# Cross-attention outputs in one score tile, the attention sink as a score column, and a new order of the output projection in a two-layer encoder

## The chip, the core and the metric

The kernel runs on one core of a Trainium2 chip. The time is the device time of one launch in microseconds (us). The core's engines are named as the profile names them: PE (TensorE, matrix multiplies and transposes; PEld is its weight load), DVE (VectorE), ACT (ScalarE), POOL (GpSimd) and SP (SyncE, which here issues nearly all DMAs). Each runs its own instruction stream in order; semaphores make one wait for another. Matrix multiplies write into PSUM, which has 8 banks of 128 partitions x 512 fp32.

## What is computed

The reference is a two-layer encoder on x of 1024 tokens x 1024 features, with 256 memory tokens. Each layer normalises its input, projects it once into all queries, keys, values and gates, runs attention groups, multiplies their outputs with SiLU gates, projects back and adds the residual. Layer 0 has a windowed group A (6 query heads, 2 key heads), a dense group B (6 and 2) and a cross-attention X into the memory (4 heads); layer 1 has a differential group C (6 heads, each with two score maps and a value twice as wide) and again X. A final normalisation follows. The part that the change touches most is the softmax with a sink in A, a learned logit per head that takes part in the softmax and has no value:

```python
    logits = jnp.where(valid[None, :, None, None], logits + bias, NEG_INF)
    sink_col = jnp.broadcast_to(sink.astype(jnp.float32).reshape(1, 1, KVH, G, 1, 1),
                                logits.shape[:-1] + (1,))
    p = jax.nn.softmax(jnp.concatenate([logits, sink_col], axis=-1), axis=-1)[..., :-1]
    out = jnp.einsum("bnkgqs,bnskd->bnqkgd", p.astype(v.dtype), vw)
```

## The kernel before

**Arithmetic.** Everything is fp32. Each operand of a projection is split into a high and a low part (`h`, `wh`, `wl` and so on), and a product is three matmuls, so most matmuls come in threes.

**PSUM.** The 8 banks are three rings (L215 to L222): `ps_s`, tag S, two tiles of 1024 columns (4 banks), for scores; `ps_t`, tag T, two tiles of 512, for transposes; `ps_a`, tag A, two tiles of 512, for accumulators. A new tile of a ring waits until the one two before it has been read out.

**Attention steps.** `run_steps` (L441) walks over a list of steps. A step takes a block of queries. `s1` writes scores into an S tile, takes the row extremum on DVE and the exponentials on ACT; `finish` divides by the row sums; `hop` copies the result by DMA from `e` to `er` (to have it in the rounded fp32 form); `s2` transposes `er` into T tiles, which ACT and DVE read out as `PTh` and `PTl`; `s3`, one step later in every pair, multiplies these with the values into an accumulator, which is read out, gated on POOL and stored. Between these parts `jobs.pull` puts in pieces of projections (`acc`, L297) that have nothing to do with the attention, as filling for PE. Scores are kept negated, so the row extremum is a minimum `mn` and exp has scale -1.

**X steps** (L570 to L634; 8 in each layer, two layers). One S tile `sx` holds four heads' scores. The odd step's `s3` is called for the head pair p=0; `s3b` is the same for p=1, with a pull between them. Each writes 8 matmuls into an A tile `ox` (L616), which ACT copies by halves (L621), DVE adds (L624) and POOL gates (L627).

**B steps** (L1040 to L1090; 48). The row minimum `mn` (L1059, DVE) is multiplied with the query's norm factor `rq` (L1063, DVE) and is then the bias `mr` of the exponential (L1064, ACT). A normalising multiply follows on POOL (L1068).

**A steps** (L1106 to L1195; 24). Each step takes two query blocks of 128 (j = 0, 1), each with a window of 384 keys, or 256 at the ends of the sequence (p = 0 and p = 3). Per block one fused DVE instruction adds the bias and takes the minimum, with the negated sink as its start value (L1132), and one exp with row sum follows (L1136). The sink's own exponential `es` is one ACT instruction for both blocks (L1139), and `finish` adds it to the row sums (L1141).

**Output projection** (`out_proj`, L1216; one per layer). It takes the 8 token tiles in the order of the table `ORD[l]`. Some tiles have been begun earlier as filling (the table `PRE`): in layer 0 tiles 2 to 5 have 24 matmuls of 48 left and tiles 6 and 7 have 12; in layer 1 tiles 2, 3 and 4 have 12 left; the others have all 48. The sums go into S tiles of 1024 columns, the last tile's into A banks (`pieces`). Then per tile: DVE adds the residual (L1274), ACT squares (L1275), DVE and POOL make the norm factor (L1283, L229), DVE scales (L1295). In layer 0 the result of a tile is transposed (`tx`, L344) after the next tile's matmuls; those of the second half of the sequence are followed by layer 1's projections (`acc`). In layer 1 it goes out by DMA.

**What sets the order.** The program is handed to a list scheduler, which chooses the order in which each engine runs its instructions, from dependencies and its own estimates. So an edit of a few lines moves instructions far from it too.

**Stages in time.** Up to 85 us: norms, transposes and first projections; 85 to 150: layer 0's X steps; 150 to 540: B and A steps; 545 to 596: output projection 0; 588 to 640: layer 1's first projections; 640 to 715: layer 1's X steps; 690 to 1180: C steps; 1180 to 1254: output projection 1.

The functions that the diff touches, with the line numbers of the profile:

Of the kernel before, what the change touches and what calls it, by code (L numbers as in the profile page):

```python
# [12 lines left out]
F32 = mybir.dt.float32  # L13
# [5 lines left out]
P = 128  # L19
# [11 lines left out]
CUTS = ((0, 4, 6, 8), (0, 4, 6, 7, 8))  # L31
LAG = 3
FAST = ("m0", "m1", "m2", "m3")
ORD = ((0, 1, 2, 3, 4, 5, 6, 7), (0, 1, 4, 2, 5, 3, 6, 7))
JORD = "xq0 m0 g6 m1 m2 g7 m3 bk bq0 bv bq1 g3 bq2 ak av aq0 g0 aq1 g4 g1 aq2 g5 g2".split()
NB0 = 1
PAT = "BBABBABBABBABBAA" * 4
# [118 lines left out]
def encoder_kernel(ctx, tc, A):  # L156
# [412 lines left out]
    def x_steps(M, X, gates, fill, qtile, ydst):  # L569
        steps = []  # L570
        for qb in range(8):
            st = Step()
            st.sub = qb % 2
            if st.sub == 0:
                grp = {}
            st.grp = grp
            e = [None]
            st.fill = fill

            def s1(qb=qb, e=e):  # L580
                kh, kl = X["kh"], X["kl"]
                Sp = ps_s("sx").rearrange("p (h m) -> p h m", h=4)
                for h in range(4):
                    qt, qc = qtile(h, qb)
                    qk(Sp[:, XPOS[h], :], qt, qc, kh[:, h, :], kl[:, h, :], 0, MEM)
                mn = stat("mn4", 4)
                nc.vector.tensor_reduce(out=mn, in_=Sp, op=ALU.min, axis=AX.X)
                et = new_e(M)
                ev = et.rearrange("p (h m) -> p h m", h=4)
                z = stat("z4", 4)  # L590
                for h in range(4):
                    nc.scalar.activation(ev[:, h, :], Sp[:, h, :], AF.Exp, bias=mn[:, h:h + 1],
                                         scale=-1.0, accum_out=z[:, h:h + 1])
                def finish():
                    rz = stat("rz4", 4)
                    nc.vector.reciprocal(rz, z)
                    for h in range(4):
                        nc.scalar.activation(ev[:, h, :], ev[:, h, :], AF.Copy, scale=rz[:, h:h + 1])
                    e[0] = et
                return finish  # L600
            st.s1 = s1
            st.hop = word_copy(M, e)
            st.s2 = dense_s2(M, e, st)
            if st.sub == 1:
                def s3(qb=qb, grp=grp, ps=(0,)):
                    v = X["v"]
                    ph, pl_ = grp["pt"]
                    for p in ps:
                        acc = ps_a("ox")
                        t = M.at.tile([P, 256], F32, tag="yt", name="yt", bufs=2)  # L610
                        for j in range(2):
                            h = 2 * p + j
                            n = 0
                            for kt in range(2):
                                for pt in (ph, pl_):
                                    nc.tensor.matmul(acc[:, j * 256:j * 256 + 256], v[:, kt, h, :],  # L616
                                                     pt[:, 2 * XPOS[h] + kt, :], start=(n == 0), stop=(n == 3))
                                    n += 1
                        for j in range(2):
                            a = slice(j * 64, j * 64 + 64)  # L620
                            nc.scalar.copy(t[a, :], acc[64 - j * 64:128 - j * 64, j * 256:j * 256 + 256])  # L621
                        for j in range(2):
                            a = slice(j * 64, j * 64 + 64)
                            nc.vector.tensor_tensor(out=t[a, :], in0=acc[a, j * 256:j * 256 + 256], in1=t[a, :],  # L624
                                                    op=ALU.add)
                        g = gates[6 + p][:, (qb - 1) * P:(qb + 1) * P]
                        nc.gpsimd.tensor_tensor(out=g, in0=t, in1=g, op=ALU.mult)  # L627
                    if qb == 7:
                        for m in ps:
                            store_y(ydst, m, gates[6 + m])  # L630
                st.s3 = s3
                st.s3b = lambda s3=s3: s3(ps=(1,))
                st.need3 = ("g6", "g7")
            steps.append(st)  # L634
        return steps
# [398 lines left out]
    if True:  # L1034
        def b_step(h, qb):
# [8 lines left out]
            def s1(h=h, qb=qb, e=e):  # L1044
# [15 lines left out]
                et = new_e(M)  # L1060
                z = stat("z")
                mr = stat("mr")
                nc.vector.tensor_tensor(out=mr, in0=mn, in1=rq[:, qb, h:h + 1], op=ALU.mult)  # L1063
                nc.scalar.activation(et, Sp, AF.Exp, bias=mr, scale=nrq[:, qb, h:h + 1], accum_out=z)  # L1064
                def finish():
                    rz = stat("rz")
# [42 lines left out]
    if True:  # L1109
        def a_step(h, p):  # L1110
# [5 lines left out]
            def s1(h=h, p=p, e=e):  # L1116
# [3 lines left out]
                    jobs.ensure("aq%d" % ((h + 1) // 2))  # L1120
                    load_q(Aq, aq_d, h + 1)
                Sp = ps_s("sa").rearrange("p (j c) -> p j c", j=2)
                et = new_e(M)[:, :768].rearrange("p (j c) -> p j c", j=2)
                mn = stat("mn2", 2)
                z = stat("z2", 2)
                for j in range(2):
                    qb = 2 * p + j
                    lo, hi = max(0, qb - 1) * P, min(8, qb + 2) * P
                    c = lo - (qb - 1) * P
                    n = hi - lo  # L1130
                    qk(Sp[:, j, c:c + n], Aq[h], qb * P, Ak["k"][h // 3], Ak["kl"][h // 3], lo, n)
                    nc.vector.tensor_tensor_reduce(out=et[:, j, c:c + n], in0=Sp[:, j, c:c + n],  # L1132
                                                   in1=abias[h][:, c:c + n], scale=1.0,
                                                   scalar=nsink[:, h:h + 1], op0=ALU.add, op1=ALU.min,
                                                   accum_out=mn[:, j:j + 1])
                    nc.scalar.activation(et[:, j, c:c + n], et[:, j, c:c + n], AF.Exp,  # L1136
                                         bias=mn[:, j:j + 1], scale=-1.0, accum_out=z[:, j:j + 1])
                es = stat("es", 2)
                nc.scalar.activation(es, mn, AF.Exp, bias=sinkb[:, h:h + 1], scale=1.0)  # L1139
                def finish():  # L1140
                    nc.vector.tensor_tensor(out=z, in0=z, in1=es, op=ALU.add)  # L1141
                    rz = stat("rz2", 2)
                    nc.vector.reciprocal(rz, z)
                    for j in range(2):
# [7 lines left out]
            st.s1 = s1  # L1152

            def hop(p=p, e=e):
                t = M.at.tile([P, 1024], F32R, tag="er", name="er", bufs=M.cfg["er"])[:, :768]
                a, b = (P if p == 0 else 0), (768 - P if p == 3 else 768)
                ef = e[0].rearrange("p j c -> p (j c)")
                dma(t[:, a:b].bitcast(F32), ef[:, a:b])
                e[0] = t.rearrange("p (j c) -> p j c", j=2)
# [56 lines left out]
    def out_proj(l, hT_next, stack):  # L1216
# [11 lines left out]
            return xr  # L1228

        def pieces(i):  # L1230
            if i < TT - 1:
                S2 = ps_s("po")
                return [(S2[:, 0:512], 0, 512), (S2[:, 512:1024], 512, 512)], [(S2, 0, 1024)]
# [354 lines left out]
```

## Time and profile before

| | |
|---|---|
| median of 3 runs | 1252.83 us (1251.51 to 1255.9) |
| profiled execution | 1255.58 us, of which the span from first to last instruction is 1253.8 us |
| PE busy | 1205.5 us (96% of the span) |
| DVE, ACT, POOL busy | 817.1, 640.2, 413.5 us (65%, 51%, 33%) |
| mean granted clock of PE | 0.996 |

Rows of the profile read as line, engine, operation, output <- inputs, shape, count, then busy time and mean duration of one, then the idle time of the engine just before such instructions and what ended it. Two matmuls that follow each other overlap, so the time from one start to the next is shorter than the listed duration. In a table of windows each engine stands with its busy time in that stretch, then PE's granted clock, the DMA share and GB/s. In the list of waits each row has the total, the number of times and the longest wait in us.

### The profile page before, as it was taken

The page shows a single profiled execution, that of the slowest core. Times are in us where ns is not written, and L with a number is a line of the kernel's source. Part 1 is how long each engine was busy: PE and PEld are TensorE (multiplying, and loading weights), DVE is VectorE, ACT ScalarE, POOL GpSimd, SP SyncE. Part 2 cuts the span into 40 slices and gives each one's busy share as a digit, 9 for nine tenths or more (in the row PEclk, how much of TensorE's full clock was granted, in tenths as well). Part 3 has the DMA queues.
Part 4 walks back from the last instruction along what each step waited for, and adds up shares of the span by engine and source line. Part 5 has one row for each costly group of instructions (what it writes and reads, how often), then busy time and mean ns, then how long its engine had stood idle before and what let it go on. Part 6 is the DMA issues. An engine that isn't in the chain of part 4 may idle for free. (4 is left out here: it accounts for less than half of the span.)

```text
span 1253.8 us, 19637 instructions
## 1 busy us (share of the span) xinstructions
PE 1205.5 (96%) x6806; PEld 999.2 (80%) x6806; DVE 817.1 (65%) x1545; ACT 640.2 (51%) x1395; POOL 413.5 (33%) x390
## 2 busy tenths in 40 slices
PE   5999999999998999998999999999999999999997
PEld 4887788888887787887888778788887878877876
DVE  5547666377778788746355865766667666678444
ACT  6249654256666766533157644444444454456322
POOL 5023456266666565403122212212122131223100
PEclk9999999999999999999999999999999999999999
DMA  6654444545365575466644334243342433445363
GB/s 252 198 187 149 155 168 150 171 155 201 148 224 191 210 246 186 154 203 213 185 163 144 125 107 120 93 143 108 105 137 76 136 115 118 144 151 189 129 211 118
DMA packets 96350, 199.90 MB, mean 159 GB/s; under 512 B 11478, under 2 KB 31190, under 8 KB 96252
## 3 DMA queue, kind: packets, MB, share of 16 engines
q1 hardware_dynamic: 96252, 198.65, 47.4%
q8 instruction: 54, 0.88, 0.3%
q14 instruction: 44, 0.36, 0.1%
HBM read 79.32 MB, written 31.47 MB: 88 GB/s over the span
## 5 line engine op out<-in xcount | busy, mean ns | idle before, releaser
L297 PE MATMUL acc<-h,wh 128*128 128x512 f32 x1536 | 499.1, 399 | 7.3 <-DVE yt L624 3.1
L297 PEld LDWEIGHTS acc<-h,wh 128*128 128x128 f32 x1536 | 283.2, 188 | 73.3 <-issue 13.4
L297 PE MATMUL acc<-h,wl 128*128 128x512 f32 x768 | 304.6, 397 | 1.8 <-POOL wl L241 1.8
L241 POOL TENSOR_TENSOR wl<-wr,wh 128x512 fp32r<-128x512 f32 x96 | 124.9, 1302 | 340.0 <-DVE wh L239 125.2
L316 DVE TENSOR_TENSOR PTl<-te,PTh 128x512 fp32r<-128x512 f32 x224 | 148.2, 687 | 131.2 <-ACT PTh L315 128.4
L1440 ACT ACTIVATE e<-e,mn 128x1024 f32<-128x1024 f32 x96 | 110.2, 1149 | 130.7 <-DVE mn L1437 127.5
L297 PEld LDWEIGHTS acc<-h,wl 128*128 128x128 f32 x768 | 144.8, 189 | 35.5 <-issue 4.4
L315 ACT CAST PTh<-te 128x512 fp32r<-128x512 f32 x224 | 124.9, 591 | 30.2 <-PE te L540 24.6
L1068 POOL TENSOR_TENSOR e<-e,rz 128x1024 f32<-128x1024 f32 x48 | 91.7, 1913 | 78.1 <-DVE rz L1067 66.7
L1437 DVE CUSTOM_DVE_ANT_0 e<-sc,toep 128x1024 f32<-128x1024 f32 x96 | 113.9, 1217 | 5.3 <-PE sc L1431 5.0
L540 PEld LDWEIGHTS te<-identr,er 128*128 128x128 f32 x896 | 91.8, 143 | 21.1 <-issue 4.1
L540 PE MATMUL te<-identr,er 128*128 128x128 f32 x896 | 100.0, 246 | 7.5 <-issue 3.2
L239 DVE CAST wh<-wr 128x512 fp32r<-128x512 f32 x112 | 59.1, 530 | 43.9 <-PE acc L297 14.4
L1064 ACT ACTIVATE e<-sb,mr,nrq 128x1024 f32<-128x1024 f32 x48 | 58.0, 1208 | 48.4 <-DVE mr L1063 33.9
L1449 DVE SCALAR_TENSOR_TENSOR e<-e,mr 128x1024 f32<-128x1024 f32 x48 | 76.2, 1588 | 1.3
L1464 PE MATMUL oc<-PTh,v 128*128 128x256 f32 x384 | 74.8, 288 | 0.3 <-DVE ckl L1333 0.3
L660 PE MATMUL po<-woh,yh 128*128 128x512 f32 (+1 forms) x172 | 65.9, 383 | 1.5 <-DVE x L1274 1.5
L660 PE MATMUL po<-woh,yl 128*128 128x512 f32 (+1 forms) x172 | 65.6, 381 | 0.0
L660 PE MATMUL po<-wol,yh 128*128 128x512 f32 (+1 forms) x172 | 65.5, 381 | 0.0
L1464 PEld LDWEIGHTS oc<-PTh,v 128*128 128x128 f32 x384 | 61.5, 192 | 0.7 <-DVE ckl L1333 0.6
L1059 DVE TENSOR_REDUCE mn<-sb 128x1 f32<-128x1024 f32 x48 | 58.4, 1216 | 5.1 <-PE sb L509 4.7
L318 ACT ACTIVATE yh<-yr 128x256 fp32r<-128x256 f32 (+2 forms) x56 | 24.0, 448 | 67.3 <-DMA yr<-ysc 38.5
(199 smaller groups left out, 2247.1 us busy)
## 6 DMA issues: line engine op xcount, KB each, us to landing
er<-e SPq DMA_DIRECT2D x112, 512.0 KB, 2.9
wr<-in_w_in SPq DMA_DIRECT2D x96, 256.0 KB, 2.8
ysc<-gy SPq DMA_DIRECT2D x16, 512.0 KB, 2.9
wor<-in_w_out SPq DMA_DIRECT2D x32, 256.0 KB, 3.5
cq<-sg SPq DMA_DIRECT2D x64, 128.0 KB, 2.6
ck<-sg SPq DMA_DIRECT2D x48, 128.0 KB, 2.3
er<-e SPq DMA_DIRECT2D x12, 384.0 KB, 2.8
xpsc<-xh SPq DMA_DIRECT2D x18, 256.0 KB, 2.5
```

The source lines that it names most:

```text
L239: nc.vector.tensor_copy(hi, raw)
L241: (nc.vector if fast else nc.gpsimd).tensor_tensor(out=lo, in0=raw, in1=hi, op=ALU.subtract)
L297: lastmm[0] = nc.tensor.matmul(acc, a, b[:, k, c0:c0 + n], start=(i == 0), stop=(i == 23))
L315: nc.scalar.copy(hi, src)
L316: return nc.vector.tensor_tensor(out=lo, in0=src, in1=hi, op=ALU.subtract)
L540: nc.tensor.transpose(to[:, i * P:(i + 1) * P], e[0][:, k * P:(k + 1) * P], idt)
L660: lastmm[0] = nc.tensor.matmul(acc, a, b, start=(start and n == 0), stop=(stop and n == 2))
L1068: nc.gpsimd.tensor_tensor(out=et, in0=et, in1=rz.to_broadcast([P, 1024]), op=ALU.mult)
L1437: nc.vector.tensor_tensor_reduce(out=et, in0=Sp, in1=toeps[h][:, w0:w0 + 1024], scale=1.0, scalar=BIG, op0=ALU.add, op1=ALU.min, accum_out ...
L1440: nc.scalar.activation(et, et, AF.Exp, bias=mn[:, m:m + 1], scale=-1.0, accum_out=z[:, m:m + 1])
L1449: nc.vector.scalar_tensor_tensor(out=es[0], in0=es[1], scalar=c, in1=es[0], op0=ALU.mult, op1=ALU.add)
L1464: nc.tensor.matmul(acc, V[:, kt, v, :], pt[:, kt, :], start=(n == 0), stop=(n == 23))
```

## The change

1. The table `ORD` gets another order of the token tiles for both layers, and the third tile in the order gets two A banks and not an S tile, so that it is read out in two halves.
2. In the X steps both head pairs' outputs go into one S tile `ox`, a half each. All 16 matmuls come first, then both halves are read out. `s3b` and the pull between are gone; the step that had them now pulls both pieces ahead of `s3`.
3. In the B steps `mr` is made on ACT (an activation with the per-row factor as scale) and not on DVE.
4. In the A steps the block in `e` gets one more column. ACT copies the negated sink there before the scores are read out: one copy of 128x2 where both windows end at the same column, two of 128x1 in the steps at the sequence's end (p = 3), 30 copies in all. The exp takes the column in, so its row sum has the sink's part. `es` and the addition to `z` are gone (24 each). The DMA of `hop` takes 769 columns and not 768.

In the changed kernel the lines up to L760 are moved by up to 3, the later ones by 2, and those behind the A steps by 5 to 8.

```diff
-ORD = ((0, 1, 2, 3, 4, 5, 6, 7), (0, 1, 4, 2, 5, 3, 6, 7))
+ORD = ((0, 1, 2, 6, 3, 7, 4, 5), (0, 1, 5, 2, 6, 3, 4, 7))
...
             if st.sub == 1:
-                def s3(qb=qb, grp=grp, ps=(0,)):
+                def s3(qb=qb, grp=grp):
                     v = X["v"]
                     ph, pl_ = grp["pt"]
-                    for p in ps:
-                        acc = ps_a("ox")
-                        t = M.at.tile([P, 256], F32, tag="yt", name="yt", bufs=2)
+                    S2 = ps_s("ox")
+                    for p in range(2):
+                        acc = S2[:, p * 512:p * 512 + 512]
                         for j in range(2):
...
+                    for p in range(2):
+                        acc = S2[:, p * 512:p * 512 + 512]
+                        t = M.at.tile([P, 256], F32, tag="yt", name="yt", bufs=2)
                         for j in range(2):
                             a = slice(j * 64, j * 64 + 64)
                             nc.scalar.copy(t[a, :], acc[64 - j * 64:128 - j * 64, j * 256:j * 256 + 256])
...
-                st.s3b = lambda s3=s3: s3(ps=(1,))
...
-                nc.vector.tensor_tensor(out=mr, in0=mn, in1=rq[:, qb, h:h + 1], op=ALU.mult)
+                nc.scalar.activation(mr, mn, AF.Identity, scale=rq[:, qb, h:h + 1])
                 nc.scalar.activation(et, Sp, AF.Exp, bias=mr, scale=nrq[:, qb, h:h + 1], accum_out=z)
...
-                et = new_e(M)[:, :768].rearrange("p (j c) -> p j c", j=2)
+                et = new_e(M)[:, :770].rearrange("p (j c) -> p j c", j=2)
...
+                ends = [(min(8, qb + 2) - qb + 1) * P for qb in (2 * p, 2 * p + 1)]
+                if ends[0] == ends[1]:
+                    nc.scalar.copy(et[:, :, ends[0]], nsink[:, h:h + 1].to_broadcast([P, 2]))
+                else:
+                    for j in range(2):
+                        nc.scalar.copy(et[:, j, ends[j]:ends[j] + 1], nsink[:, h:h + 1])
...
-                    nc.scalar.activation(et[:, j, c:c + n], et[:, j, c:c + n], AF.Exp,
+                    nc.scalar.activation(et[:, j, c:c + n + 1], et[:, j, c:c + n + 1], AF.Exp,
                                          bias=mn[:, j:j + 1], scale=-1.0, accum_out=z[:, j:j + 1])
-                es = stat("es", 2)
-                nc.scalar.activation(es, mn, AF.Exp, bias=sinkb[:, h:h + 1], scale=1.0)
                 def finish():
-                    nc.vector.tensor_tensor(out=z, in0=z, in1=es, op=ALU.add)
...
-                a, b = (P if p == 0 else 0), (768 - P if p == 3 else 768)
+                a, b = (P if p == 0 else 0), (769 - P if p == 3 else 769)
...
         def pieces(i):
+            if i == 2:
+                p = [(ps_a("po")[:, 0:512], c, 512) for c in (0, 512)]
+                return p, p
             if i < TT - 1:
```

What the scheduler makes of it stands in the order of the instructions. The first place is PE in layer 0's X steps, at the third pair. `ox` is the output of the attention, `acc` a projection, `te` a transpose of a finished step's `er`, and the numbers tell tiles apart. Before:

```order
L616 MATMUL ox_1440<-PTh_1247,xv_410 128x256
L616 MATMUL ox_1440<-PTl_1249,xv_410 128x256
L297 MATMUL acc_1492<-h_120,wh_1212 128x512
L297 MATMUL acc_1492<-h_121,wh_1212 128x512
L297 MATMUL acc_1492<-h_120,wl_1213 128x512
```

In the changed kernel:

```order
L616 MATMUL ox_1424<-PTh_1246,xv_410 128x256
L616 MATMUL ox_1424<-PTl_1248,xv_410 128x256
L297 MATMUL acc_1490<-h_121,wh_1197 128x512
L297 MATMUL acc_1490<-h_120,wl_1198 128x512
L793 MATMUL ssq_1406<-small_80,sq_1399 128x2 x4
L540 MATMUL te_1457<-identr_74,er_1278 128x128 x4
L540 MATMUL te_1464<-identr_74,er_1278 128x128 x4
```

The second pair's output (`ox_1440`) used to take the A bank whose turn the projection's `acc_1492` shares; now all of `ox_1424` is in an S tile, the projection has begun in the middle of it, and the transposes `te`, which stood ahead of the second pair's output, come behind it.

The second place is PE in layer 1, where the last X steps meet the first C steps. `sc` are the two score maps of a C step (m = 0, 1), each an S tile; the matmuls with `ckl` have 64 rows, and those of the two maps can run side by side. Before:

```order
L616 MATMUL ox_7922<-PTl_7809,xv1_6875 128x256
L540 MATMUL te_7941<-identr_74,er_7848 128x128 x4
L540 MATMUL te_7948<-identr_74,er_7848 128x128 x4
L1425 MATMUL sc_7967<-ck0_7494,cq_7734 128x512 x2
L1431 MATMUL sc_7967<-ckl_7496,cq_7734 128x512
L1425 MATMUL sc_7968<-ck1_7495,cq_7737 128x512 x2
L1431 MATMUL sc_7968<-ckl_7496,cq_7737 128x512
L1431 MATMUL sc_7967<-ckl_7496,cq_7734 128x512
L1431 MATMUL sc_7968<-ckl_7496,cq_7737 128x512
L297 MATMUL acc_7996<-h_6327,wh_7675 128x512
```

In the changed kernel, in two pieces five rows apart (the rows between are of `acc`):

```order
L616 MATMUL ox_7865<-PTh_7765,xv1_6835 128x256
L616 MATMUL ox_7865<-PTl_7767,xv1_6835 128x256
L1433 MATMUL sc_7924<-ck0_7454,cq_7693 128x512 x2
L1439 MATMUL sc_7924<-ckl_7456,cq_7693 128x512 x2
L297 MATMUL acc_7953<-h_6281,wl_7635 128x512
L297 MATMUL acc_7953<-h_6281,wh_7634 128x512
```

```order
L297 MATMUL acc_7953<-h_6281,wl_7641 128x512
L1433 MATMUL sc_7925<-ck1_7455,cq_7696 128x512 x2
L1439 MATMUL sc_7925<-ckl_7456,cq_7696 128x512 x2
L297 MATMUL acc_7953<-h_6281,wh_7640 128x512
L297 MATMUL acc_7953<-h_6282,wh_7640 128x512
```

Each of the two score maps now stands by itself, with a projection's matmuls between them, since `ox_7865` holds one of the two S tiles until it has been read out. Three C steps stand so in the changed kernel, one did before.

The third place is ACT at an A step followed by a B step. Before:

```order
L315 CAST PTh<-te 128x4x128
L1136 ACTIVATE e,z_3146<-e,mn_3145 128x384
L1136 ACTIVATE e,z_3146<-e,mn_3145 128x256
L1139 ACTIVATE es<-mn_3145,small 128x2
L437 COPY yt<-ob 64x256
L315 CAST PTa<-ta 128x3x128 x2
L1064 ACTIVATE e,z<-sb,mr,nrq 128x1024
```

In the changed kernel:

```order
L315 CAST PTh<-te 128x4x128
L1133 COPY e<-nsink 128x1 x2
L1144 ACTIVATE e,z_3136<-e,mn_3135 128x385
L1144 ACTIVATE e,z_3136<-e,mn_3135 128x257
L437 COPY yt<-ob 64x256
L315 CAST PTa<-ta 128x3x128 x2
L1065 ACTIVATE mr<-mn,rq 128x1
L1066 ACTIVATE e,z<-sb,mr,nrq 128x1024
```

`es` is gone, the sink's copies stand ahead of the two exps, and `mr` stands ahead of the dense step's exp.

More of the change, by code (lines that the diff above doesn't have):

```diff
@@ L628, in s3 @@
                     if qb == 7:
-                        for m in ps:
+                        for m in range(2):
                             store_y(ydst, m, gates[6 + m])
                 st.s3 = s3
-                st.s3b = lambda s3=s3: s3(ps=(1,))
                 st.need3 = ("g6", "g7")
@@ L1154, in hop @@
             def hop(p=p, e=e):
-                t = M.at.tile([P, 1024], F32R, tag="er", name="er", bufs=M.cfg["er"])[:, :768]
-                a, b = (P if p == 0 else 0), (768 - P if p == 3 else 768)
+                t = M.at.tile([P, 1024], F32R, tag="er", name="er", bufs=M.cfg["er"])[:, :770]
+                a, b = (P if p == 0 else 0), (769 - P if p == 3 else 769)
                 ef = e[0].rearrange("p j c -> p (j c)")
```

## The prediction

> **What bounds the kernel now.** I began with the busy time per 100 us, to see where PE has anything left to lose.
>
> ```profile
> 300.00:400.00 100.00, 97.73 (x602) 83.55 (x600) 75.87 (x172) 65.24 (x148) 63.07 (x59) 1.00 0.51 181
> 400.00:500.00 100.00, 92.74 (x570) 78.10 (x570) 81.66 (x178) 68.82 (x151) 58.97 (x52) 0.98 0.63 222
> 500.00:600.00 100.00, 95.19 (x514) 79.19 (x513) 62.03 (x117) 41.96 (x95) 28.58 (x32) 1.00 0.59 192
> 800.00:900.00 100.00, 100.00 (x564) 80.93 (x563) 69.28 (x121) 47.69 (x95) 21.60 (x22) 1.00 0.34 113
> ```
>
> After the two window bounds and their length comes PE. It is the bound everywhere; in the C steps (800 to 900) it is never idle, and the change leaves them alone. It can only give back PE's idle time elsewhere: 2.3 + 7.3 us between 300 and 500, 4.8 us around output projection 0, and some in the X steps. The list of PE's waits says what ends that idle time.
>
> ```profile
> PE te L540 <- issue: 3.2, 5, 1.4
> PE acc L297 <- DVE yt L624: 3.1, 2, 1.8
> PE sa L509 <- ACT e L1064: 2.1, 2, 1.1
> PE sa L509 <- DVE mn L1132: 1.7, 3, 1.1
> PE tx L344 <- DVE h L316: 1.7, 1, 1.7
> PE po L660 <- DVE x L1274: 1.5, 1, 1.5
> PE pre L660 <- DVE yt L438: 1.2, 1, 1.2
> PE tx L344 <- DVE xs L1295: 1.2, 2, 0.7
> PE acc L297 <- DVE v L1283: 1.1, 1, 1.1
> ```
>
> No wait is large. The change aims at several of these rows: `yt L624` (A banks in the X steps), `e L1064` (exponential of B behind `mr`), and the `po`, `tx` and `acc` rows of the output projections. All nine make 16.8 us: even with every one of them gone the kernel would be 1.3% faster.
>
> **Layer 0's X steps.** A projection's `acc` waits twice for an A bank that DVE (L624) has not read out. The change takes `ox` out of the A banks, so these 3.1 us have no cause left. But look at what ACT does there (fourth engine in the row, after PE, PEld and DVE), and how long the read-out lasts:
>
> ```profile
> 110.00:120.00 10.00, 8.75 (x54) 7.35 (x52) 6.59 (x14) 9.80 (x28) 1.47 (x2) 1.00 0.77 205
> 120.00:130.00 10.00, 8.92 (x62) 7.89 (x60) 7.36 (x13) 9.85 (x26) 7.66 (x6) 1.00 0.46 160
> 130.00:140.00 10.00, 9.26 (x39) 7.57 (x40) 5.03 (x11) 7.34 (x20) 1.97 (x2) 0.83 0.53 180
> 130.74 1.10 PE L297 MATMUL acc<-h,wh 128*128 128x512 f32 x2 [1.82 <-DVE yt L624]
> L621 ACT COPY yt<-ox 64x256 f32<-64x256 f32 x32 | 11.7, 367 | 0.7
> L624 DVE TENSOR_TENSOR yt<-ox,yt 64x256 f32<-64x256 f32 x32 | 13.4, 420 | 2.6 <-ACT yt L621 1.7 <-issue 0.5
> ```
>
> From 110 to 130 ACT idles 0.35 us. What runs through ACT (exponentials, divisions, `PTh`) cannot come sooner by more than that; PE can only run ahead with projections, and then meets the transposes `te` of a step whose division is not done. And the S ring now carries `ox` as well: an S tile with `ox` is held for four copies and four adds, 4 x 0.367 + 4 x 0.420 = 3.1 us if ACT and DVE do not overlap. So the bounds are a gain of 3.1 us and, with one read-out uncovered, a loss of 3.1 us. I take a gain of 1: the A-bank wait is certain to go, most of it should reappear at `te`.
>
> **B and A steps.** DVE loses 48 `mr` and 24 additions, ACT gets 48 `mr` and 30 sink copies and loses 24 `es`:
>
> ```profile
> L1063 DVE TENSOR_TENSOR mr<-mn,rq 128x1 f32<-128x1 f32 x48 | 9.3, 193 | 0.7
> L1141 DVE TENSOR_TENSOR z<-z,es 128x2 f32<-128x2 f32 x24 | 6.9, 286 | 14.0 <-ACT es L1139 13.9
> L1139 ACT ACTIVATE es<-mn,small 128x2 f32<-128x2 f32 x24 | 6.8, 281 | 0.0
> L1483 ACT ACTIVATE z<-ssqc,es 128x1 f32<-128x1 f32 x48 | 10.0, 258 | 4.5 <-PE ssqc L1479 4.3
> ```
>
> DVE is relieved of 9.3 + 6.9 = 16.2 us. No row has ACT's new operations; nearest is L1483, one column with a per-row operand, 0.258 us. That makes 48 x 0.258 + 30 x 0.258 - 6.8 = 13.3 us more on ACT. Over the 390 us of these steps DVE is the busier engine (76 and 82% against 65 and 69%), so the load moves the right way. One `mr` is 0.258 - 0.193 = 0.065 us dearer there, 48 x 0.065 = 3.1 us if every one lay on the path. [...]
>
> Whether a `mr` is on the path is decided by queues. DVE's in-order queue did this to one of them:
>
> ```profile
> 394.38 3.64 DVE L258 TENSOR_TENSOR wol<-wor,woh 128x512 fp32r<-128x512 f32 x1
> 397.94 0.15 DVE L1063 TENSOR_TENSOR mr<-mn,rq 128x1 f32<-128x1 f32 x1
> 398.12 1.21 ACT L1064 ACTIVATE e<-sb,mr,nrq 128x1024 f32<-128x1024 f32 x1 [2.48 <-DVE mr L1063]
> 399.47 0.44 PE L509 MATMUL sa<-ak,q 128*128 128x384 f32 x1 [0.98 <-ACT e L1064]
> 401.43 0.50 PE L540 MATMUL te<-identr,er 128*128 128x128 f32 x4 [1.35 <-issue]
> ```
>
> DVE had just taken the minimum, a weight split of 3.64 us came between it and `mr`, ACT stood idle for 2.48 us, and PE paid 0.98 us for the S tile that this exp held and, as I read it, 1.35 us behind it. With `mr` on ACT the exp no longer queues behind DVE's split. Against these 2.3 us stand the exps where ACT is the late one: each starts up to 0.26 us later. Three such on PE's path make 0.8. I take a gain of 1.5. Bounds: the five rows of waits of these steps (`te` 3.2, `sa` 2.1 and 1.7, `pre` 1.2) all gone, 8.2; or the 11 waits in them each longer by one `mr` and one copy, 11 x 0.52 = 5.7 lost. The sink's copies stand ahead of DVE's minimum on the same tile; ACT is normally free by then, and I cost them at nothing; were they late, they would be in these 5.7. `es` and its addition leave the division's chain, which ends in a DMA that PE meets a step later: nothing. The 769th column lengthens a DMA that lands steps ahead of its use: nothing.
>
> **Output projections.** The chain behind a tile, against a matmul's pitch (0.23 us between the first two starts):
>
> ```profile
> L1274 DVE TENSOR_TENSOR x<-po,xr 128x1024 f32<-128x1024 f32 (+2 forms) x19 | 20.0, 1053 | 17.5 <-PE po L660 13.4 <-issue 3.2 <-DMA x1sc<-x 0.8
> L1275 ACT ACTIVATE xs<-x 128x1024 f32<-128x1024 f32 (+1 forms) x16 | 16.1, 1008 | 14.8 <-DVE x L1274 7.8 <-DVE yl L319 3.5 <-issue 1.8
> L1295 DVE SCALAR_TENSOR_TENSOR xs<-x,r,gb 128x1024 f32<-128x1024 f32 (+1 forms) x16 | 20.0, 1251 | 10.5 <-POOL r L229 10.4
> 1209.32 0.39 PE L660 MATMUL po<-wol,yh 128*128 128x512 f32 x1
> 1209.55 0.39 PE L660 MATMUL po<-woh,yl 128*128 128x512 f32 x1
> 1211.43 0.47 PE L660 MATMUL po<-woh,yh 128*128 128x512 f32 x1 [1.49 <-DVE x L1274]
> ```
>
> From a tile's last matmul to its transposes lie at least 1.05 + 1.01 + 1.25 = 3.3 us and the small operations. A short tile (12 matmuls) covers 12 x 0.23 = 2.7 us, one of 24 covers 5.5, a full one 10.9. In layer 0 the two short tiles stood last, and 1.2 + 1.1 + 1.7 = 4.0 us of waits (`tx`, `acc`, `tx`) lie at this place. With the order 0, 1, 2, 6, 3, 7, 4, 5 the two tiles ahead of a short one (2 and 3) are still badly covered; the last one is now long, its first half is read out while the second runs, and layer 1's start has its bank. So the 1.1 us should go, and a little of the others: gain 1.4, bounds 0 and 4.0. In layer 1 two short tiles followed 0 and 1 directly, and the fifth waited 1.49 us for an S tile. Now the third is a full one in A banks, and every S tile that is reused has a long one or an idle DVE ahead: gain 1.5, bounds 0 and 1.5.
>
> **Layer 1, where X meets C.** A C step's 64-row matmuls cost less when those of two maps alternate:
>
> ```profile
> 690.03 0.73 PE L1431 MATMUL sc<-ckl,cq 64*128 64x512 f32 x2
> 690.69 0.50 PE L616 MATMUL ox<-PTh,xv 128*128 128x256 f32 x2
> 704.68 0.73 PE L1431 MATMUL sc<-ckl,cq 64*128 64x512 f32 x4
> 705.34 0.73 PE L297 MATMUL acc<-h,wh 128*128 128x512 f32 x2
> ```
>
> Two alone take 690.69 - 690.03 = 0.66 us, four alternating take the same 0.66. In the changed order three C steps are torn apart and not one: 2 x 0.66 = 1.3 us lost. The waits of the second map for `ox`'s read-out come on top, 0 to 3.1; the A-bank waits of these steps go, under 1. I take a loss of 0.5; bounds 1 gained, 4 lost.
>
> **The sum.** -1 - 1.5 - 1.4 - 1.5 + 0.5 = -4.9, against a profiled execution of 1255.58: 1250.7. That execution lay 2.75 above the median of 1252.83, so the median after is 1252.83 - 4.9 = 1247.9, 0.4% faster. About 0.3% (3.8 us, 1249.0) is what a measurement can tell from no change.
>
> **The rivals.** *The gains are given back.* ACT is the pacer in the X steps and PE waits at `te` for what it saved; in the B and A steps the earlier and the later exps cancel. Then only the output projections and the torn C steps count: -1.4 - 1.5 + 1.3 = -1.6, 1251.2. For it: ACT's 0.35 us of idle. Against it: DVE's queue at 394. If instead every `mr` on ACT is paid for on the path, the sum is without the 1.5 and with 3.1: 1247.9 + 1.5 + 3.1 = 1252.5; and if no edit does what it says, it stays at 1252.8. All three are within 0.3% and share one chance.
>
> *The clock.* One more row, beside 130 to 140 above:
>
> ```profile
> 430.00:440.00 10.00, 9.35 (x51) 7.85 (x51) 8.23 (x20) 7.48 (x17) 6.64 (x6) 0.83 0.71 247
> ```
>
> In both windows the granted clock is 0.83, which loses 10 x 0.17 = 1.7 us each, and one begins right behind the wait at 130.74. If the change removes both waits' idle time and makes no new one, 3.4 us more are gained: 1244.5. But the waits at 401 and 1211 drew no such drop, so it hangs on chance. [...]
>
> *Slower: a ring of two.* `ox` in the S ring leaves the scores one tile, in the steps that need it most; in six of the eight cross outputs (the first of each layer has no queue) the next scores or map wait for the read-out as long as the A-bank waits lasted, 3.1 / 2 = 1.55 us: 6 x 1.55 = 9.3. With the other terms (-1.5 - 1.4 - 1.5 + 1.3, -3.1) that is 1259. It decides from 3.1 / 6 = 0.5 us per output up. For it: ACT at 98%, the torn maps. Against: seven or more of a projection's matmuls (7 x 0.23 = 1.6 us) stand between in the order.
>
> **How the numbers follow.** Forecast 0.45 (1247.9, own range 1245 to 1251), gains given back 0.25 (1251.2), clock 0.14 (1244.5), ring 0.16 (1259). Faster by over 0.3%: three quarters of the forecast, the clock, a little of the second: 0.50. Slower: nearly all of the ring: 0.15. Within: 0.35. The range 1243 to 1256 leaves out the clock's lower end and most of the ring.
>
> **What would show it.** Right: no `acc <- yt L624` in the list of waits; the exp near 398 starts about 2 us earlier and `sa` behind it no longer waits; no wait of `po` near 1211; three pairs of 64-row matmuls at 0.66 us around 700. Wrong: PE waits of 1 us or more at `te` between 110 and 150 or at `sc` around 700; more waits `<- ACT e` in the B steps than the two of before; a granted clock below 1 in windows that had 1.

## The result, and the profile after

The changed kernel took 1242.89 us (median of 6 runs, 1241.58 to 1244.78) against 1254.37 us of the kernel before beside it (1251.51 to 1257.93): a ratio of 0.9910, 95% interval 0.9895 to 0.9925. In a later set on one chip the same two stood at 0.9893 (0.9877 to 0.9909). So it is 0.9 to 1.1% faster, on the side that was forecast and more than twice as far as the 0.4% of the forecast. The measured 1242.89 us is below the forecast's own range of 1245 to 1251 and 0.1 us below the lower end of the whole range, 1243 to 1256.

The profiled execution took 1241.79 us with a span of 1240.0, 13.8 us less than before. To see where, I counted PE's matmuls by their pitch and compared the two traces at equal amounts of work done. (Each kind of matmul counts with its usual time from one start to the next, its pitch. This is worked out from the records of one trace each; it leaves shifts of a few tenths, since the order differs.)

| stretch, by the clock of the kernel before | gain in the traces | forecast |
|---|---|---|
| 100 to 161 us: X steps of layer 0 | 5.6 us | 1.0 |
| 161 to 530: B and A steps | 2.7 | 1.5 |
| 530 to 640: output projection 0, first projections of layer 1 | 0.2 | 1.4 |
| 640 to 749: X steps of layer 1 into the C steps | 3.0 | -0.5 |
| 749 to 1173: C steps | 0.1 | 0 |
| from 1173: output projection 1 | 2.2 | 1.5 |
| sum | 13.8 | 4.9 |

The two stretches with X steps have 8.6 us of it, where 0.5 was expected. Of the 13.8 us, 10.5 are idle time of PE and 3.3 are busy time, which fell from 1205.5 to 1202.2. First the sums of the changed kernel, then its busy time per 100 us (PE is the first number behind the length):

```profile
PE 1202.2 (97%) x6806; PEld 999.9 (81%) x6806; DVE 805.7 (65%) x1479; ACT 651.9 (53%) x1453; POOL 412.1 (33%) x390
```

```profile
100.00:200.00 100.00, 99.57 (x585) 84.83 (x584) 67.17 (x114) 74.56 (x168) 50.40 (x41) 1.00 0.45 159
300.00:400.00 100.00, 97.52 (x608) 85.19 (x607) 76.75 (x149) 69.77 (x166) 66.03 (x59) 0.98 0.56 197
400.00:500.00 100.00, 93.25 (x576) 78.89 (x575) 77.08 (x156) 70.76 (x167) 59.26 (x52) 0.98 0.59 210
500.00:600.00 100.00, 96.39 (x501) 79.45 (x500) 57.97 (x103) 37.65 (x85) 22.93 (x28) 1.00 0.61 193
700.00:800.00 100.00, 99.46 (x549) 79.50 (x547) 66.36 (x122) 46.83 (x92) 23.02 (x23) 1.00 0.34 116
```

Between 300 and 500, PE is nearly as idle as it was (2.5 + 6.8 us, before 2.3 + 7.3). PE's list of waits in the changed kernel, by its longest rows behind the start-up:

```profile
PE tx L344 <- DVE xs L1303: 3.2, 5, 1.2
PE te L540 <- issue: 2.5, 1, 2.5
PE ob L1083 <- ACT PTh L315: 2.4, 1, 2.4
PE ob L1083 <- DVE PTl L316: 1.2, 2, 0.6
PE oa L1192 <- DVE yt L438: 1.1, 1, 1.1
```

`acc <- DVE yt`, `sa <- ACT e`, `po <- DVE x`, `acc <- DVE v` and `tx <- DVE h` are gone. In their place stand three rows that were short or absent: `tx <- DVE xs` (1.2 in 2 before), `ob <- ACT PTh` and `ob <- DVE PTl`. And this is the same stretch as the one that the prediction took for paced by ACT:

```profile
110.00:120.00 10.00, 9.69 (x60) 8.09 (x59) 7.03 (x14) 9.68 (x26) 3.76 (x5) 1.00 0.70 206
120.00:130.00 10.00, 10.00 (x69) 9.05 (x68) 6.90 (x11) 9.43 (x24) 4.00 (x4) 1.00 0.45 158
130.00:140.00 10.00, 10.00 (x54) 7.84 (x52) 7.76 (x16) 8.73 (x25) 2.78 (x3) 1.00 0.43 160
```

ACT is still 94 to 97% busy up to 130, and PE is idle for 0.3 us of these 30, where it was idle for 3.1. The granted clock is 1.00 at 130, where it was 0.83.

### The profile page after: what moved, and what is told of

The parts are those of the page before. It is cut to its first block, busy times and chain, and to the rows that moved or that the text cites. A ratio compares the mean times of both kernels' runs of the same rounds, so it can differ in the third digit from the quotient of the medians.

```text
span 1240.0 us, 19680 instructions
## 1 busy us (share of the span) xinstructions
PE 1202.2 (97%) x6806; PEld 999.9 (81%) x6806; DVE 805.7 (65%) x1479; ACT 651.9 (53%) x1453; POOL 412.1 (33%) x390
## 5 line engine op out<-in xcount | busy, mean ns | idle before, releaser
L239 DVE CAST wh<-wr 128x512 fp32r<-128x512 f32 x112 | 56.3, 504 | 42.1 <-PE acc L297 17.8
```

## The experiments

### Which part is worth how much

The first set undoes one part or does one alone. Undoing the second part (the cross outputs back into the A banks, one call per head pair):

```diff
-                    S2 = ps_s("ox")
-                    for p in range(2):
-                        acc = S2[:, p * 512:p * 512 + 512]
+                    for p in ps:
+                        acc = ps_a("ox")
...
+                st.s3b = lambda s3=s3: s3(ps=(1,))
```

> All of the change except its second part: the cross outputs stay in the A banks, one call per head pair. Theory 1 (by the stages of the two traces: the X steps of layer 0 gave 5.6 us and those of layer 1 some 2 to 3): without it 8 us of the 11.5 are gone, about 1251, ratio to the kernel before 0.997, and the two waits of the projection for the A bank (1.25 and 1.82 us) and a granted clock below 1 near 130 us are back. Theory 2 (the prediction's: ACT paces the X steps, so this part is worth 0.5 us and the rest came from elsewhere): about 1243.5, ratio 0.991 to 0.992.

Measured: 1249.77 us, ratio to the kernel before 0.9956 (0.9942 to 0.9971). So the part is worth 0.9956 - 0.9910, 0.46% or 5.8 us. Theory 2 falls, and the 8 us of Theory 1 were too much. In the trace against the kernel before, the stretch of layer 0's X steps has gained 1.6 us by 188 us (the full change: 5.8), and layer 1's, from 640 to 749, 1.4 (full: 3.0). Both waits for the A bank are back, at the same places, but the clock is not:

```profile
117.03 0.70 PE L297 MATMUL acc<-h,wh 128*128 128x512 f32 x2 [1.24 <-DVE yt L624]
130.90 0.70 PE L297 MATMUL acc<-h,wh 128*128 128x512 f32 x2 [1.82 <-DVE yt L624]
```

```profile
130.00:140.00 10.00, 9.10 (x47) 7.65 (x48) 5.68 (x11) 7.88 (x21) 2.06 (x3) 1.00 0.52 170
```

The same idle times 0.2 us later than in the kernel before, and 1.00 where that one had 0.83. So the drop at 130 us does not follow from the wait alone, and the 1.6 us by which this kernel is ahead there fit its absence (1.7 us). Without the clock the part is worth 5.8 - 1.6 = 4.2 us in layer 0: the 3.1 us of the two waits and about 1 more, whose cause no row shows.

The second part alone, put into the kernel before (the diff of point 2 and nothing else):

> The kernel before with only the second part: the cross outputs in one S tile per pair of steps. Theory 1: 8 us faster than the kernel before, about 1246, ratio 0.993 to 0.994, no wait of the projection for the A bank, clock 1.0 from 100 to 200 us. Theory 2 (worth 0.5 us): ratio 0.999 to 1.000. A third way: the gain needs the other parts, because the scheduler orders the whole differently; then the ratio lies between and the stage to 150 us alone shows the gain.

Measured: 1247.65 us, ratio 0.9938 (0.9915 to 0.9962), 7.8 us faster. Theory 1. In the trace it has gained 5.9 us by 188 us and 2.6 from 640 to 749; output projection 1 gave nothing (7.4 us ahead at 1173, 7.2 at 1227), where the full change and the first experiment gained 2.1 over the same stretch.

The third part undone (`mr` back on DVE):

```diff
-                nc.scalar.activation(mr, mn, AF.Identity, scale=rq[:, qb, h:h + 1])
+                nc.vector.tensor_tensor(out=mr, in0=mn, in1=rq[:, qb, h:h + 1], op=ALU.mult)
```

> All of the change except its third part: the product for the dense steps' exponential stays on DVE. Theory 1: the queue of DVE was what cost PE 0.98 and 1.35 us near 400 us, so 1 to 2.5 us come back: about 1244.5, ratio to the kernel before 0.992 to 0.993. Rival: ACT's 48 x 0.26 us cost more on the path than DVE's queue, so this kernel is faster than the full change, ratio 0.989 or less. Third: no difference beyond the interval, 0.991, since the scheduler fills PE with projections either way.

Measured: 1243.92 us, ratio 0.9911 (0.9890 to 0.9932). The third expectation: no difference from the full change that these intervals can tell.

The fourth part undone (`es` and its addition back, no sink column):

```diff
-                    nc.scalar.activation(et[:, j, c:c + n + 1], et[:, j, c:c + n + 1], AF.Exp,
+                    nc.scalar.activation(et[:, j, c:c + n], et[:, j, c:c + n], AF.Exp,
...
+                nc.scalar.activation(es, mn, AF.Exp, bias=sinkb[:, h:h + 1], scale=1.0)
...
+                    nc.vector.tensor_tensor(out=z, in0=z, in1=es, op=ALU.add)
```

> All of the change except its fourth part: the windowed steps keep the sink's own exponential and its addition, and no sink column. Theory 1: the part saves 24 x (0.28 + 0.29) us on ACT and DVE, costs 30 copies on ACT, and is off PE's path: ratio 0.990 to 0.992 as the full change. Rival: the shorter chain behind the windowed exponentials is worth 1 to 2 us of the B and A stage's 2.4: ratio 0.992 to 0.993.

Measured: 1242.05 us, ratio 0.9897 (0.9876 to 0.9919). Theory 1 in that nothing is lost; the ratio lies just below its range.

### Both of these together, and the output projections

Parts 3 and 4 both undone (the last two diffs):

> The kernel before with parts 1 and 2 alone (new tile order with the third tile in A banks, cross outputs in score tiles); the product stays on DVE and the sink keeps its exponential. Theory 1 (the runs with one of them undone lay at 0.9911 and 0.9897, the full change at 0.9910): parts 3 and 4 together are worth 0 to 1 us, ratio to the kernel before 0.990 to 0.992. Rival (the B and A stage gained 2.3 us between the two traces, and that is theirs): ratio 0.9925 to 0.993.

Measured: 1243.64 us, ratio 0.9913 (0.9896 to 0.9929), in Theory 1's range: parts 3 and 4 together are worth between nothing and 2 us (0.9913 against 0.9910 in one set and 0.9893 in another), and the intervals do not settle where. PE's waits from 300 us to the end of the A steps got no shorter. Without the two parts:

```profile
PE te L540 <- issue: 2.6, 4, 1.3
PE sa L509 <- ACT e L1066: 2.0, 2, 1.0
PE pre L662 <- DVE yt L438: 1.2, 1, 1.2
PE oa L1189 <- DVE yt L438: 0.9, 1, 0.9
```

All rows of that answer add up to 8.4 us, those of the full change in the same stretch to 9.2. But the count of matmuls from 161 to 530 us tells the kernels apart: the ten traces with `mr` on ACT gain 1.0 to 3.2 us there over the kernel before, the three with `mr` on DVE (this one, the one with only the third part undone and the one with the second part alone) -1.0 to 0.4. So the third part seems to be worth about 2 us in this stretch, in shorter times between matmuls and not in the listed waits; no row shows through what. The fourth part shows no gain there (2.8 and 3.0 in the two traces without it).

In the list of waits, the one for the exponential goes and others come. The trace of the full change shows how, at the step that stood at 398 in the kernel before. First ACT, then DVE, then PE:

```profile
385.90 0.30 ACT L1065 ACTIVATE mr<-mn,rq 128x1 f32<-128x1 f32 x1
386.28 1.21 ACT L1066 ACTIVATE e<-sb,mr,nrq 128x1024 f32<-128x1024 f32 x1
```

```profile
383.98 1.22 DVE L1061 TENSOR_REDUCE mn<-sb 128x1 f32<-128x1024 f32 x1
385.11 4.57 DVE L258 TENSOR_TENSOR wol<-wor,woh 128x512 fp32r<-128x512 f32 x2
389.60 0.15 DVE L1069 RECIPROCAL rz<-z 128x1 f32<-128x1 f32 x1
391.12 1.27 DVE L316 TENSOR_TENSOR PTl<-te,PTh 128x512 fp32r<-128x512 f32 x2
```

```profile
391.89 0.51 PE L540 MATMUL te<-identr,er 128*128 128x128 f32 x4 [2.48 <-issue]
```

The minimum is done at 383.98 + 1.22 = 385.20 and the exp starts 1.1 us later, where it had taken 3.7 us: that is what the third part is there to do. But two weight splits still hold DVE for 4.57 us, and now the reciprocal and, behind an addition and the next minimum, the low parts `PTl` in the same queue are what is late. The transposes start when the first of the two `PTl` is done, near 391.12 + 1.27 / 2 = 391.8; that they waited for it is read from the times, since the row names no releaser. PE idles 2.48 us there in one piece, where it had idled 0.98 + 1.35 in two.

The old order of tiles in layer 0's output projection, with its third tile in an S tile again, everything else as in the full change:

```diff
-ORD = ((0, 1, 2, 6, 3, 7, 4, 5), (0, 1, 5, 2, 6, 3, 4, 7))
+ORD = ((0, 1, 2, 3, 4, 5, 6, 7), (0, 1, 5, 2, 6, 3, 4, 7))
...
-            if i == 2:
+            if i == 2 and l == 1:
```

> The full change, but layer 0's output projection keeps the old order of tiles and its third tile in an S tile; layer 1's is the new. Theory 1 (by the two traces this place nets 0 to 0.8 us: one wait of 1.1 us for a bank went, and the waits at the transposes for the scaled tile grew from 1.2 in 2 to 3.2 us in 5): ratio 0.990 to 0.9915. Rival (the prediction's 1.4 us): ratio 0.992 to 0.9925.

Measured: 1243.57 us, ratio 0.9913 (0.9896 to 0.9931): Theory 1. The old waits are back,

```profile
PE tx L344 <- DVE h L316: 1.6, 1, 1.6
PE tx L344 <- DVE xs L1303: 1.1, 2, 0.7
PE acc L297 <- DVE v L1291: 1.1, 1, 1.1
```

3.8 us in place of the new order's 3.2 at the transposes: layer 0's new order is worth about half a microsecond, below what can be told.

The third tile of both output projections in an S tile, the new orders kept:

```diff
-            if i == 2:
-                p = [(ps_a("po")[:, 0:512], c, 512) for c in (0, 512)]
-                return p, p
```

> The full change, but the third tile of both output projections is in an S tile as before; the new orders stay. Theory 1 (the order alone does it: no short tile follows another with a reused S tile): no wait of po over 1 us, ratio 0.990 to 0.9915. Rival (the A banks are needed): the third tile is a full one and starts right behind the last 6 matmuls (1.4 us) of the second, while the first one's S tile needs 1.2 us of read-out and more; 0.5 to 2 us are lost in each layer, ratio 0.992 to 0.9935, with a po wait of that size.

Measured: 1241.71 us, ratio 0.9895 (0.9876 to 0.9914), and no `po` wait in the trace: Theory 1, a little below its range. The order does it; the A banks for the third tile are not needed.

### Where the gain of the X steps comes from

The score tile in layer 0 alone, layer 1's cross outputs in the A banks:

```diff
+                if ydst == 0:
                     def s3(qb=qb, grp=grp):
...
+                else:
+                    def s3(qb=qb, grp=grp, ps=(0,)):
...
+                    st.s3b = lambda s3=s3: s3(ps=(1,))
```

> The full change, but layer 1's cross outputs stay in the A banks; layer 0's are in score tiles. Theory 1 (the second part gains in both layers, in layer 1 by 1.6 to 2.8 us in the traces): ratio 0.9923 to 0.9932. Rival (the prediction's: in layer 1 it tears two more pairs of score maps apart at 0.66 us each and lends S tiles away, so without it the kernel is faster): ratio 0.990 or less, with the paired 64-row matmuls back.

Measured: 1245.08 us, ratio 0.9925 (0.9910 to 0.9940), against 0.9910 and 0.9893 for the full change: 1.9 to 4 us. The first of these intervals overlaps this run's, the second ends just below it. In the trace it loses 2.4 us to the full change from 640 to 749. Theory 1. The whole list of PE's waits in that stretch:

```profile
PE te L540 <- DVE v L316: 1.7, 1, 1.7
PE ox L648 <- ACT e L598: 0.6, 1, 0.6
PE ox L648 <- DVE yt L656: 0.6, 2, 0.3
```

The kernel before has the same three, 2.4 us in all, the last two shorter,

```profile
PE te L540 <- DVE v L316: 1.7, 1, 1.7
PE ox L616 <- DVE yt L624: 0.5, 2, 0.3
PE ox L616 <- ACT e L598: 0.2, 1, 0.2
```

and the full change has none of them. It does pay for the torn pairs of score maps as predicted: three of its C steps have the 64-row matmuls of each map alone, 0.66 us for two:

```profile
683.53 0.73 PE L1439 MATMUL sc<-ckl,cq 64*128 64x512 f32 x2
684.19 0.39 PE L616 MATMUL ox<-PTh,xv 128*128 128x256 f32 x1
```

So against this run 2.9 us of waits go and 1.3 come, as two more pairs are torn than in the kernel before: 1.6, of the 2.4 in the trace.

Then a set with the full change on the same chip, which stood there at 1241.45 us, 0.9893 (0.9877 to 0.9909):

> The changed kernel once more, so that the three others of this set have it on the same chip. All theories: ratio to the kernel before 0.990 to 0.992. Near 130 us the granted clock is 1; whether a window between 300 and 500 us is at half clock may differ from the first profile, if the drops hang on when a wait falls and not on the kernel alone.

As expected, and with drops of the clock at the same two places as in its first profile. Beside it, ACT's copies of layer 0's cross outputs done twice, to ask whether ACT paces that stage:

```diff
+                            for _ in range(2 if ydst == 0 else 1):
-                            nc.scalar.copy(t[a, :], acc[64 - j * 64:128 - j * 64, j * 256:j * 256 + 256])
+                                nc.scalar.copy(t[a, :], acc[64 - j * 64:128 - j * 64, j * 256:j * 256 + 256])
```

> The full change with each of ACT's 16 half-tile copies of layer 0's cross outputs done twice (the same values, 16 x 0.37 = 6 us more on ACT between 100 and 150 us, and each score tile held 0.7 us or more longer). Theory 1 (PE has projections to run and the S tile is free long before it is needed; ACT does not pace the stage): at most 1 us lost, ratio 0.990 to 0.992. Rival (the prediction's: ACT is busy 98% and paces the stage): 4 to 6 us lost, ratio 0.994 to 0.9955, with PE waits at the transposes or scores between 100 and 150 us.

Measured: 1245.60 us, ratio 0.9929 (0.9913 to 0.9945), 4.1 us more than the full change on the same chip. Neither expectation holds whole: more is lost than Theory 1 allows, and the rival has the loss and a wait for a score tile right, but not the ratio. By the traces 1.9 us of it are lost in the stage itself, out of 16 x 0.37 = 6 us added; so ACT does not set the pace of the stage, though it is not far from it. The rest is lost behind 400 us, where by the names of the tiles each engine runs the order of the full change (the orders differ only between 112 and 172 us); its cause stays open. In the stage PE now waits once for a score tile:

```profile
119.03 0.35 PE L509 MATMUL sx<-xkh,q 128*128 128x256 f32 x1 [1.17 <-ACT e L592]
118.03 0.86 DVE L628 TENSOR_TENSOR yt<-ox,yt 64x256 f32<-64x256 f32 x2 [1.46 <-ACT yt L625]
```

The first row names an exponential as the releaser, but the additions that read `ox` out of this tile end at 118.03 + 0.86 = 118.89, 0.14 us before the matmul. This is the ring of two of the slower rival. It begins to bite when the tile is held longer; in the full change it does not. There the tile that `ox` left at 108 us is read out by 115.3 and needed at 119.8 (PE, ACT, DVE, PE):

```profile
108.01 0.28 PE L616 MATMUL ox<-PTl,xv 128*128 128x256 f32 x1
```

```profile
113.61 0.75 ACT L624 COPY yt<-ox 64x256 f32<-64x256 f32 x2
```

```profile
114.39 0.86 DVE L627 TENSOR_TENSOR yt<-ox,yt 64x256 f32<-64x256 f32 x2
```

```profile
119.78 0.28 PE L509 MATMUL sx<-xkh,q 128*128 128x256 f32 x1
```

So there is 4.5 us of slack (1.6 us at the least among layer 0's four outputs), and the read-out, whose second half begins 5.6 us after the matmuls, holds up nobody.

Last of this kind, the halves of the one S tile called one after the other again, each with its own read-out and a pull between:

```diff
-                def s3(qb=qb, grp=grp):
+                def s3(qb=qb, grp=grp, ps=(0,)):
-                    S2 = ps_s("ox")
+                    if 0 in ps:
+                        grp["ox"] = ps_s("ox")
+                    S2 = grp["ox"]
...
+                st.s3b = lambda s3=s3: s3(ps=(1,))
```

> The full change, but the two head pairs are called one after the other as before, each with its own read-out and a projection piece between them; both still use the halves of one S tile. Theory 1 (the gain comes from taking the outputs out of the A banks): ratio 0.990 to 0.992. Rival (the gain comes from doing all 16 matmuls at once and from the merged pull): 3 to 7 us lost, ratio 0.9935 to 0.9965.

Measured: 1247.38 us, ratio 0.9939 (0.9924 to 0.9953), 5.9 us more than the full change beside it. Each theory has one half. In layer 0's X steps almost nothing is lost (0.2 us by 161), so there the gain comes from leaving the A banks. In layer 1 4.0 us are lost from 640 to 749, more than with A banks; 2.3 of them are waits that the full change does not have, at `ox` (1.0 and 0.3) and at `te` (1.0). About 1 us more is lost between the two stretches, with no cause shown. PE, and the DVE additions it waits for:

```profile
660.50 0.36 PE L619 MATMUL ox<-PTh,xv 128*128 128x256 f32 x1 [1.00 <-ACT e L598]
```

```profile
659.50 0.86 DVE L627 TENSOR_TENSOR yt<-ox,yt 64x256 f32<-64x256 f32 x2 [0.59 <-ACT yt L624]
```

The second pair's matmuls start at 660.50, right after the additions that read out the first pair's half, at 659.50 + 0.86 = 660.36. The row names an ACT instruction of the division as the releaser, which does not touch this tile; the additions end 0.14 us before the matmul starts. The two halves are different banks but one tile, and the second half waited here until the first had been read out: in all eight pairs of this trace its matmuls start 0.14 us or more behind these additions. In the kernel before, with an A tile for each, two of the eight start ahead of them (127.81 against 130.59, and 692.02 against 694.33). With all 16 matmuls first there is nothing to wait for. Whether the two pulls put together have a share in layer 1's gain, no run separates.

### A version to beat both

The full change without its sink column and with the third tile in an S tile (the diffs above):

> The full change without its sink column and with the third tile of the output projections in an S tile. Theory 1 (both were neutral or slightly faster alone, 0.9897 and 0.9895): ratio 0.988 to 0.990, 1 to 2 us faster than the full change on the same chip. Rival (both differences were chance): 0.9905 to 0.992 as the full change.

Measured: 1242.28 us, ratio 0.9900 (0.9884 to 0.9915), beside the full change's 0.9893: no faster than the full change on the same chip, as the rival had it, though both ratios are below the rival's range. Neither is faster than the other, and no version of these runs is told apart from the full change on the good side.

## Why the prediction was right in sign and too small

**What bounds the kernel** stood: PE, with the C steps untouched (0.1 us over 420 us). What the list of waits allowed (16.8 us) was not passed; 11.5 us is well below. But it was not the limit that it was taken for: 3.3 of the profile's 13.8 us came out of PE's busy time, which no wait lists. Of the signs named beforehand all four for "right" came, and one of the three for "wrong": a lower clock in a window that had 1, at 390.

**Layer 0's X steps: the step that failed.** The prediction took 1 of 3.1 us, because "what runs through ACT cannot come sooner by more than that" and the wait "should reappear at `te`". It did not. The changed kernel's trace has no `te` wait in that stage, and PE was filled with projections. 4.2 us are measured for the part without the clock (the first experiment against the full change), all of the two waits and 1 us more. The false step is to read ACT's busy share as a pace. ACT's queue held work that was urgent only while the output sat in an A bank; once it sits in a tile with 1.6 us of slack or more the copies can come late. The doubled copies show the size: of 6 us more on an engine called full, 1.9 were lost in the stage.

**The clock** was a rival of its own at 0.14, and its 1244.5 is the nearest of the named times to the 1242.89 measured. That is chance. Of its two places one came true: the drop at 130 us is gone in every kernel with the score tile there, 1.7 us (and in the first experiment, which has the old wait). But the other, near 430, stayed and a new one came near 390, behind the 2.48 us wait of `te`: two drops before, two after. So the clock moved within the sum and gave nothing net. It also makes the B and A stretch, with one drop more than before, look 1.7 us worse than it would at full clock.

**B and A steps.** 1.5 was taken, with 0 to 2 us found for parts 3 and 4 by the times and about 2 for the third by the traces, so the size was about right. The way to it was not. DVE's split ahead of `mr` was seen rightly, and the exp no longer queues behind it; but the instructions behind `mr` in the same DVE queue stay late, and the 2.3 us that PE should have won near 398 came back as 2.48. By the count, the gain lies in shorter times between matmuls, which the prediction did not look at, and their cause is open. (Its "five rows" of waits are four; their sum of 8.2 is right.) `mr` itself costs more on ACT than the 0.258 us assumed, the copies less:

```profile
L1065 ACT ACTIVATE mr<-mn,rq 128x1 f32<-128x1 f32 x48 | 14.1, 295 | 42.4 <-DVE mn L1061 42.0
L1130 ACT COPY e<-nsink 128x2 f32<-128x2 f32 x18 | 3.5, 201 | 0.4 <-DMA er<-e 0.4
L1133 ACT COPY e<-nsink 128x1 f32<-128x1 f32 x12 | 1.8, 200 | 0.0
```

14.1 + 3.5 + 1.8 - 6.8 = 12.6 us more on ACT, 13.3 were estimated. One `mr` takes 0.295 us on ACT, where it took 0.193 on DVE. On which of the two it belongs the times do not settle: with `mr` on DVE the kernel ran at 0.9911, within the interval of the full change (0.9895 to 0.9925). The count of matmuls (1.0 to 3.2 us gained with `mr` on ACT, -1.0 to 0.4 with it on DVE) speaks for ACT in this case.

**Output projections.** Layer 1's term was right in cause and place: the `po` wait went by the order, 2.1 us with what came behind it, 1.5 forecast. Layer 0's term failed: the `acc` wait of 1.1 went as said, but "a little of the others" did not go with it; the `tx` waits grew to 3.2 us, so 0.6 or less was left of 1.4. And of the two means in this part, the A banks for the third tile were not needed.

**Layer 1, where X meets C.** The torn pairs cost their 1.3 us, as worked out. The other side of that term was mis-sized: the waits that the change takes away here were put at "under 1". They were 1.7 (`te <- DVE v`), which I had quoted and then given to nobody, and 0.7 at `ox`. And no wait for a torn map's tile came. So the loss of 0.5 should have been a gain of 1.7 + 0.7 - 1.3 = 1.1 by these rows; the traces show 1.6 to 3.0 (3.0 against the kernel before, 2.4 and 1.6 against the two runs with layer 1's outputs in A banks), outside the bound of 1 gained, and the rest has no row.

**The rivals.** "Gains given back" held for layer 0's order and for the waits of the B and A steps, not for the whole. The ring of two did not decide: PE stood idle for no score tile in the full change, and the doubled copies brought one such wait of 1.2 us.

## What to carry to other kernels

A busy share near 100% on an engine did not make it the pace-setter of a stage here (ACT, 94 to 97% busy in the full change, was given 6 us more, and 1.9 were lost): ask which of its instructions somebody waits for, and whether a tile that is needed again later lets the others come late. A wait that is quoted has to be given a fate in the sum, gone or kept, also where the change seems to be about something else. Moving one short instruction out of a long in-order queue freed what hung on it (the exp starts 1.1 us behind the minimum, where it took 3.7) and left the next one in that queue to be waited for (2.48 us of PE's time); and the second half of one tile waited for the first, 1.0 us at 660.50, even in different banks, so write both before reading either.

## What was not expected of the hardware

PE's clock drops (0.83 to 0.84 in a window of 10 us, 3.4 us at half rate, 1.7 us lost) came in 13 of the 14 profiles, none to three in each while PE had work: in the kernel before at 130 and 430 us, in the full change twice at 390 and 430, with the cross outputs back in the A banks only at 390. Equal idle times at an equal place drew a drop in one kernel (1.82 us at 130.74) and none in another (1.82 us at 130.90).

Two traces give the idle time ahead of each drop. In the kernel before the drops start at 130.83 and 431.21 us, in the full change at 392.27 and 433.24, and each lasts 3.413 us at a granted clock of 0.50. In the 3.41 us just ahead PE idled for 1.82 and 2.24 us, and for 2.48 and 1.55, so it was not idle throughout. Idle times as long as these drew no drop at other places: the pair of waits near 400 in the kernel before, 0.98 + 1.35 us, and in the full change a wait of 2.36 us ahead of a matmul of `ob` at 424.76. In the last run above (no sink column, third tile in an S tile) PE idled for as much as 3.09 us between 420 and 430, and the granted clock stayed at 1.00 there and in the 10 us behind. So within one trace 1.55 us drew a drop and 2.36 us drew none: the length of the idle time alone does not decide. The prediction's "hangs on chance" holds that far; what else decides is left open here.

One profile's difference of 1.7 us is therefore no evidence for an edit until the clock of the window has been read.
